# Scores of split vectors: a second pass over all 128 rows, and values split in every key block

## The chip, the cores and the metric

The kernel runs on one core of a Trainium2 chip. The metric is the device time of one execution in microseconds (us), smaller being better; the time before is the median of three runs.

## The reference, cut to what matters

The program is a two-layer encoder trunk with 512 tokens of 1024 features, all in float32. A layer is a feed-forward block, three token mixers that run on one normalised input and are merged by gates, and a second feed-forward block. The mixers are A (differential attention, 4 heads with two score products each), B (attention over a band of chunks with a table of biases, 8 heads) and C (retention, 4 heads with decay in place of softmax). The lines that the change touches compute the scores of A, B and C and the values of B:

```python
s = jnp.einsum('bqhcd,bkhcd->bhcqk', qi, k) * scale          # A, 4 heads x 2
s = jnp.einsum('bnqhd,bnkhd->bnhqk', qc, kb) * scale + bias  # B, 8 heads
o = jnp.einsum('bnhqk,bnkhd->bnqhd', p, vb)                  # B, values
inner = jnp.einsum('bnqhd,bnkhd->bnhqk', qc, kc) * decay     # C, 4 heads
```

Heads of q and k are 64 features wide; B's values are 64 wide, A's and C's 128.

## The kernel before, in words

**Split numbers.** Nearly all products run in a reduced float32 format (fp32r), and each operand is written as hi + lo to keep accuracy. A product of two split operands is three passes of TensorE (hi·hi, hi·lo, lo·hi). The large projections, the feed-forward blocks and the branch products go this way: one weight tile `wr` of 128x1024 arrives by DMA, ScalarE makes its hi (`wh`), VectorE its lo (`wl`), and 24 passes use the two. Three raw tiles and three split ones are in turn (RAW and SPL, lines 186 and 187). Where the diff has no say this is the "main program".

**Scores.** A head of q or k has only 64 features, and TensorE sums over up to 128 partitions, so hi and lo are stacked. `stack` (line 650; `c_prep`, line 996, for C) builds for each head a tile `qk` whose two halves of the partitions hold hi and lo of q, or hi twice for k, by DMAs from SBUF to SBUF on the queue of SyncE (SP). `dots` (line 664) then needs two passes. The first runs over all 128 rows and gives hi·hi + hi·lo. The second multiplies hi of q with lo of k; in the kernel before it takes one half of the partitions, 64 rows, straight from the tile `ql` that VectorE wrote (the tile `kl` in C). `scores` calls `dots` for a block of 128 queries with 256, 256, 384 and 512 keys in turn; C does the same with q and k exchanged.

**Values of B.** `evac_vb` (line 570) leaves the first three blocks of keys as pairs of tiles in which a head's hi and lo stand side by side (`vv`), the fourth as one tile in plain float32 (`v`). In `values_b` (line 591) the first three blocks take a pass 128 columns wide and one 64 columns wide; the fourth takes one plain float32 product with 64 columns of the values, which the trace records as two entries.

**What sets the order.** Heads and preparations are generators, "side programs". After each pass of the main program `tick` (line 249) may run one step of them. Which step is due is decided when the program is built, by `Model`, which estimates when each engine is through: a pass costs it n / 2.37 ns whatever its rows, a tile that DMAs fill counts as ready 2.5 us after `sent`, and a score waits 0.8 us more (`MARGIN`). Each engine and each queue then runs its own list in order. The requests for weights and the DMAs of `stack` share SP's queue. `b_head` for heads 0 and 1 starts once the first pair of k is sent, so its first scores come soon after those DMAs.

```python
    def dots(self, out, lhs, rhs):
        self.nc.tensor.matmul(out=out, lhsT=lhs[0], rhs=rhs[0], start=True, stop=False)
        self.nc.tensor.matmul(out=out, lhsT=lhs[1], rhs=rhs[1], start=False, stop=True)
```

Of the kernel before, what the change touches and what calls it, by code (L numbers as in the profile page):

```python
# [18 lines left out]
P = 128  # L19
S = 512  # L20
# [11 lines left out]
# columns of the per-partition constants  # L32
# [3 lines left out]
class Queue:  # L36
    """An engine's instructions, with an estimate of when each ends: side programs are woven in by it."""
# [14 lines left out]
class Model:  # L52
    """Estimates of when each engine is through with what it was given, and of which banks of PSUM are free."""
# [13 lines left out]
    def ready(self, ap, eng="pe"):  # L67
        """When an engine can read it."""
        end, by = self.wrote.get(self.key(ap), (0.0, eng))
        if by == eng:  # L70
            return end + (0 if eng == "pe" else 127)
        return end + self.LAG[by]
# [7 lines left out]
    def free(self, ap):  # L80
        """Its last reader is on the way."""
        end, by = max(self.read.get(self.key(ap), [(0.0, "pe")]))
        self.slots[self.owner.pop(self.key(ap))] = end + self.LAG[by]

    def sent(self, ap, wait=2500):
        """A transfer into it starts now."""
        self.wrote[self.key(ap)] = max(self.t.values()) + wait, "pe"
# [35 lines left out]
def then(*aps):  # L123
    """Wait: for a step of the vector or scalar engine."""
    return aps, False, 0


def product(*aps):
    """Wait: for a step of the tensor engine."""
    return aps, False, Kernel.EASE  # L130


def room(*aps):
    """Wait: for a step that takes a bank of PSUM."""
    return aps, True, Kernel.MARGIN


class Kernel:
# [26 lines left out]
    # ---------------------------------------------------------------- tiles  # L165
# [23 lines left out]
    # ------------------------------------------------- the stream of weights  # L189
# [39 lines left out]
    # ------------------------------------------------------- side programs  # L229
# [19 lines left out]
    def tick(self):  # L249
        """After a product of the main program: a step of a side program, where one is due."""  # L250
        m = self.model
        if self.late and m.ready(self.late[0][0], "dve") <= max(m.t["dve"], m.t["pe"]):
            self.late.pop(0)[1]()
        if self.prio and self.step(self.prio):
            return
        t = self.model.t
        if t["pe"] < self.due or max(t["dve"], t["act"]) > t["pe"] + self.BACKLOG:
            return
        self.admit()
        before = t["pe"]  # L260
        if self.step(self.active):
            self.due = t["pe"] + self.PACE * (t["pe"] - before)
# [17 lines left out]
    def step(self, lst):  # L280
        """Run the first program whose operands the tensor engine would not wait for."""
        for e in lst:
            if e[3] is not None and e[3] not in self.flags:
                continue
            if e[0] > self.model.t["pe"] or e[4] and min(self.model.slots) > self.model.t["pe"]:
                continue
            e[3] = None
            try:
                w = next(e[1])
            except StopIteration:  # L290
                lst.remove(e)
                return True
            if isinstance(w, str):
                e[3], e[4] = w, True
            else:
                aps, e[4], more = w
                e[0] = max([self.model.ready(a) for a in aps], default=0) + more
            return True
        return False
# [13 lines left out]
    # -------------------------------------------------------------- helpers  # L313
    def rsqrt(self, src, n, mul, add, final=None):
        """final / sqrt(src * mul + add), [P, n]."""
# [13 lines left out]
    def rsqrt_wide(self, y, src, mul, add, final=None):  # L329
        """y = final / sqrt(src * mul + add), [P, S], in steps."""  # L330
# [15 lines left out]
    def total(self, bank, parts):  # L346
        """Sums over the partitions, in every partition."""
        for i, x in enumerate(parts):
            self.nc.tensor.matmul(out=bank, lhsT=self.ones, rhs=x, start=i == 0, stop=i == 1)

    def split2(self, src, s):
        """hi and lo of a tile in SBUF."""
# [13 lines left out]
    # ------------------------------------------------------------- the norm  # L366
    def norm_part(self, k, gcol):
        """x[k] is final: its share of the sum of squares and its split for the next products."""
# [26 lines left out]
    def norm_rows(self):  # L395
        """rb, 1 / rms(x) by token in every partition."""
# [8 lines left out]
    def settle(self):  # L405
        """The urgent programs to their ends."""
# [4 lines left out]
    def norm_tokens(self):  # L411
        """rb, and rt with the tokens in partitions."""
# [10 lines left out]
    # ------------------------------------------------------------------ FFN  # L423
    def proj(self, xs, n=KD):
        """One output tile of features: a bank with its n products."""
# [7 lines left out]
    def open(self, xs):  # L433
        """The first two output tiles, side by side, as x and the weights come in."""
# [76 lines left out]
    # ---------------------------------------------------------------- mixer  # L511
    def tokens(self, evac, first=False):
        """512 columns of the projection with tokens in partitions."""
# [56 lines left out]
    def evac_vb(self, v):  # L570
        """The values of B: a head's hi and lo side by side."""
        nc = self.nc

        def f(b, bank):
            r = self.rt[:, b:b + 1]
            if b == NB - 1:
                t = self.big(F32, "v")
                nc.scalar.activation(out=t, in_=bank, func=AF.Copy, scale=r)
                v.append(t)
                return  # L580
# [10 lines left out]
    def values_b(self, pt, v, h):  # L591
        """A head's sum over the keys in the first half of a bank's partitions, but for the part of the values' lo, in the other."""
        o = self.bank()
        mm = self.nc.tensor.matmul
        for j in (0, 1, NB - 1, 2):
            if j == NB - 1:
                yield product(pt[j], v[j])
                mm(out=o[0:64, j * P:S], lhsT=v[j][:, h * 64:(h + 1) * 64], rhs=pt[j], start=False, stop=False)
                continue
# [10 lines left out]
    def prep(self, z, ms, out, flag, tabs=None, final=None, gain=None):  # L610
        """Norm and rotation of q or k (tokens in partitions), then the transposes and splits."""
# [38 lines left out]
    def stack(self, parts, out, flag):  # L650
        """Two heads of q or k, [2 * 64, tokens], split: for each head hi in its own half of the partitions
        and lo in the other (q), or hi twice (k), and what the second pass takes (hi of q, lo of k)."""
# [3 lines left out]
        for r, other in zip(half, half[::-1]):  # L656
            t = self.big(F32R, "qk")
            for o, x in ((r, hi), (other, lo if is_q else hi)):
                self.nc.sync.dma_start(out=t[o].bitcast(F32), in_=x[r].bitcast(F32))
            self.model.sent(t)  # L660
            out.append((t, (t if is_q else lo)[r]))
        self.flags.add(f"{flag}{len(out) // 2 - 1}")

    def dots(self, out, lhs, rhs):
        """Products of split vectors: of the stacked parts in one pass, of what is left in another."""
# [10 lines left out]
    def softmax(self, bank, i, add, s, e):  # L676
        """exp(scores + add - max) into e and the sums into s; add is [P, 512], aligned at its end."""
# [8 lines left out]
    def weights(self):  # L686
        """Room for the weights [q, k] of four blocks of queries."""
# [3 lines left out]
    def turned(self):  # L691
        """Room for the weights' transposes, by blocks of keys: [k, q], hi and lo."""
# [4 lines left out]
    def transposed(self, es):  # L697
        """Weights [q, k] of four blocks of queries -> per block of keys their transposes, split."""
# [20 lines left out]
    def values(self, pt, v, cols):  # L719
        """Sum over the keys: [values, queries] in a bank."""  # L720
# [10 lines left out]
    def settle_head(self, o, st, h):  # L731
        """A head's values out of PSUM, and the sums of their squares by token, in a half of the partitions."""
# [17 lines left out]
    def finish(self, st, heads, gains, final, gate, out, flag):  # L750
        """The norm over a head's values, its gains and its gate."""
# [134 lines left out]
    def table(self):  # L886
        """The next head's table of biases or decays."""
# [83 lines left out]
    def c_tables(self):  # L971
        """cos and sin, by the norm."""
# [6 lines left out]
    def rotated(self, tabs):  # L979
        """q or k of C, the first and the second halves of the four heads' features."""  # L980
# [15 lines left out]
    def c_prep(self, halves, out, s):  # L996
        """The split, and for each head hi in a half of the partitions and lo in the other (q), or hi twice (k),
        and what the second pass takes (hi of q, lo of k)."""
# [4 lines left out]
        for h in range(4):  # L1003
            hi, lo = ([p[i][32 * h:32 * h + 32] for p in parts] for i in range(2))
            t = self.big(F32R, "qk")
            a, b = h % 2 * 64, 64 - h % 2 * 64
            if s == "k" and h % 2 == 0:
                low = self.big(F32R, "kl")
            moves = [(t, a, hi), (t, b, hi if s == "k" else lo)]
            if s == "k":  # L1010
                moves.append((low, a, lo))
            for to, at, pieces in moves:
                for i, x in enumerate(pieces):
                    self.nc.sync.dma_start(out=to[at + 32 * i:at + 32 * i + 32].bitcast(F32), in_=x.bitcast(F32))
                self.model.sent(to)
            out.append((t, (low if s == "k" else t)[a:a + 64]))
# [64 lines left out]
    # ------------------------------------------------------------------ all  # L1081
# [132 lines left out]
```

## Time and profile before

| what | value |
|---|---|
| median of 3 runs | 2588.64 us (2587.83 to 2589.02) |
| span of the profiled execution | 2586.1 us |
| own time of the profiled execution | not given apart from the span; the median is 2.5 us above it |
| TensorE busy, passes | 2575.3 us, 11226 |
| VectorE busy | 1380.5 us, 53% |
| ScalarE busy | 921.3 us, 36% |
| granted TensorE clock, mean | 1.000 |

The span runs from the first to the last instruction. Matmuls overlap each other, and their ends are modelled, so a duration of a matmul is longer than the time that it keeps the next one waiting; the distance from start to start tells what a pass costs. A weight load (PEld) stands ahead of each pass and runs beside the pass before it where it can. In the timeline `128*64` behind an operation is rows times columns of the part of the array that is used, and `x2` a merged row.

### The profile page before, as it was taken

What the parts mean: (1) busy time and instruction counts of PE and PEld (TensorE: products, weight loads), DVE (VectorE), ACT (ScalarE), POOL (GpSimd) and SP (SyncE); (2) the same over time, 40 slices, a digit from 0 to 9 for tenths busy, and PEclk for the clock granted to TensorE, in tenths of its full rate; (3) what the DMA queues carried; (4) which work ended last, traced back from release to release, by engine and by line L of the source; (5) the groups of instructions that cost most, each with busy time, mean ns of one, the idle gap of its engine ahead of it and who ended that gap; (6) DMA issues with size and microseconds to landing.
All of it is one profiled execution on the core that took longest, in us unless ns stands there. A gap on an engine that the chain in (4) does not pass through costs nothing.

```text
span 2586.1 us, 28788 instructions
## 1 busy us (share of the span) xinstructions
PE 2575.3 (100%) x11226; PEld 2047.4 (79%) x11226; DVE 1380.5 (53%) x2176; ACT 921.3 (36%) x1395; POOL 133.8 (5%) x104
## 2 busy tenths in 40 slices
PE   9999999999999999999999999999999999999999
PEld 7888887777777888888888888877777778888887
DVE  6444347667658653343353343476776586544332
ACT  4333224544443333332232332245444433333321
POOL 0000101000102100000000001010001021000000
PEclk9999999999999999999999999999999999999999
DMA  4333335236422433333332323352364234333332
GB/s 164 98 94 94 118 118 142 78 86 157 121 81 82 131 98 98 98 98 92 97 97 90 98 90 118 113 151 70 89 161 122 71 90 130 98 94 94 98 110 70
DMA packets 90728, 271.46 MB, mean 105 GB/s; under 512 B 12256, under 2 KB 13664, under 8 KB 90592
## 3 DMA queue, kind: packets, MB, share of 16 engines
q1 hardware_dynamic: 89872, 269.01, 35.1%
q8 instruction: 88, 1.44, 0.2%
q10 hardware_dynamic: 720, 0.62, 0.1%
q14 instruction: 48, 0.39, 0.1%
HBM read 237.08 MB, written 6.29 MB: 94 GB/s over the span
## 4 chain that ended last, share of the span: by engine, by line
PE 99%; DVE 0%; DMA 0%; ACT 0%; issue 0%; SPq 0%
PE bank L48 99%; DVE z L48 0%; DMA x<-in_xt 0%; DMA w<-in_w 0%; ACT wh L48 0%; DVE xl L48 0%; DVE x L48 0%; DVE t L48 0%; ACT xh L48 0%; SPq L1109 0%; SPq L1107 0%; DVE wl L48 0%
## 5 line engine op out<-in xcount | busy, mean ns | idle before, releaser
L48 DVE TENSOR_TENSOR wl<-wr,wh 128x1024 fp32r<-128x1024 f32 x422 | 528.7, 1254 | 709.4 <-ACT wh L48 708.2
L48 PE MATMUL bank<-xh,wh 128*128 128x512 f32 x1920 | 762.3, 397 | 0.0
L48 PE MATMUL bank<-xh,wl 128*128 128x512 f32 x1920 | 759.2, 395 | 0.0
L48 PE MATMUL bank<-xl,wh 128*128 128x512 f32 x1920 | 757.1, 394 | 0.3 <-DVE xl L48 0.3
L48 ACT ACTIVATE wh<-wr 128x1024 fp32r<-128x1024 f32 x422 | 445.4, 1056 | 786.1 <-PE bank L48 674.5
L48 PEld LDWEIGHTS bank<-xh,wl 128*128 128x128 f32 x1920 | 361.2, 188 | 84.4 <-issue 3.8
L48 PEld LDWEIGHTS bank<-xl,wh 128*128 128x128 f32 x1920 | 361.3, 188 | 81.0 <-issue 2.2
L48 PEld LDWEIGHTS bank<-xh,wh 128*128 128x128 f32 x1920 | 361.5, 188 | 79.7 <-issue 1.8
L48 PE MATMUL bank<-ph,wh 128*128 128x512 f32 x704 | 277.6, 394 | 0.0
L48 PE MATMUL bank<-ph,wl 128*128 128x512 f32 x704 | 276.2, 392 | 0.0
L48 PE MATMUL bank<-pl,wh 128*128 128x512 f32 x704 | 275.9, 392 | 0.0
L48 PE MATMUL bank<-wh,xh 128*128 128x512 f32 x448 | 182.2, 407 | 0.0
L48 PE MATMUL bank<-wl,xh 128*128 128x512 f32 x448 | 181.9, 406 | 0.0
L48 PE MATMUL bank<-wh,xl 128*128 128x512 f32 x448 | 180.4, 403 | 0.0
L48 PEld LDWEIGHTS bank<-ph,wl 128*128 128x128 f32 x704 | 132.4, 188 | 30.6
L48 PEld LDWEIGHTS bank<-pl,wh 128*128 128x128 f32 x704 | 132.4, 188 | 29.1
L48 PEld LDWEIGHTS bank<-ph,wh 128*128 128x128 f32 x704 | 132.5, 188 | 28.8
L48 ACT ACTIVATE e<-e,m 128x128 f32<-128x128 f32 (+3 forms) x128 | 71.7, 560 | 136.4 <-DVE m L48 126.1
L48 ACT ACTIVATE t<-t 128x512 f32<-128x512 f32 x88 | 55.6, 632 | 162.4 <-DVE t L48 162.4
L48 PEld LDWEIGHTS bank<-wh,xh 128*128 128x128 f32 x448 | 84.2, 188 | 22.4 <-issue 4.3
L48 PEld LDWEIGHTS bank<-wh,xl 128*128 128x128 f32 x448 | 84.3, 188 | 20.4 <-issue 2.4
L48 PEld LDWEIGHTS bank<-wl,xh 128*128 128x128 f32 x448 | 84.4, 188 | 19.9 <-issue 2.1
(149 smaller groups left out, 2466.8 us busy)
## 6 DMA issues: line engine op xcount, KB each, us to landing
wr<-in_w SPq DMA_DIRECT2D x422, 512.0 KB, 3.5
qk<-qh SPq DMA_DIRECT2D x96, 128.0 KB, 4.6
xd<-x SPq DMA_DIRECT2D x16, 256.0 KB, 2.5
tb<-in_tbias SPq DMA_DIRECT2D x16, 256.0 KB, 3.8
qk<-ql SPq DMA_DIRECT2D x32, 128.0 KB, 4.3
rh<-r SPq DMA_DIRECT2D x32, 128.0 KB, 4.7
x<-xd SPq DMA_DIRECT2D x16, 256.0 KB, 5.3
qk<-yh SPq DMA_DIRECT2D x48, 64.0 KB, 2.0
```

What stands on the lines that cost most here:

```text
L48: return call(*args, **kw)
```

## The change

The second pass of the scores gets operands over all 128 partitions. For k, a second tile is built with lo in both halves, by two DMAs a head as for the first tile (in C four, where there were two into a tile shared by two heads). For q the whole tile is used, hi in one half and lo in the other. The pass then yields lo·hi + lo·lo in place of lo·hi. `twice` is new and holds what stood in the loop of `stack`. In B the fourth block of values is written as hi and lo side by side like the others, and its plain float32 product takes 128 columns in place of 64, so that the other half of the bank receives the part of lo. The order of all engines is worked out anew by `Model`. The diff also removes comments and docstrings, which shifts line numbers.

```diff
 def evac_vb(self, v):
...
-            if b == NB - 1:
-                t = self.big(F32, "v")
-                nc.scalar.activation(out=t, in_=bank, func=AF.Copy, scale=r)
-                v.append(t)
-                return
             two = [self.big(F32R, "vv") for _ in range(2)]
...
 def values_b(self, pt, v, h):
...
             if j == NB - 1:
-                yield product(pt[j], v[j])
-                mm(out=o[0:64, j * P:S], lhsT=v[j][:, h * 64:(h + 1) * 64], rhs=pt[j], start=False, stop=False)
+                t = v[j][h // 4][:, h % 4 * P:(h % 4 + 1) * P]
+                yield product(pt[j], v[j][h // 4])
+                mm(out=o[:, j * P:S], lhsT=t.bitcast(F32), rhs=pt[j], start=False, stop=False)
                 continue
...
 def stack(self, parts, out, flag):
...
         for r, other in zip(half, half[::-1]):
-            t = self.big(F32R, "qk")
-            for o, x in ((r, hi), (other, lo if is_q else hi)):
-                self.nc.sync.dma_start(out=t[o].bitcast(F32), in_=x[r].bitcast(F32))
-            self.model.sent(t)
-            out.append((t, (t if is_q else lo)[r]))
+            t = self.twice(hi[r], lo[r] if is_q else hi[r], r, other)
+            out.append((t, t if is_q else self.twice(lo[r], lo[r], r, other)))
         self.flags.add(f"{flag}{len(out) // 2 - 1}")
 
+    def twice(self, a, b, own, other):
+
+        t = self.big(F32R, "qk")
+        for o, x in ((own, a), (other, b)):
+            self.nc.sync.dma_start(out=t[o].bitcast(F32), in_=x.bitcast(F32))
+        self.model.sent(t)
+        return t
...
 def c_prep(self, halves, out, s):
...
-            t = self.big(F32R, "qk")
             a, b = h % 2 * 64, 64 - h % 2 * 64
-            if s == "k" and h % 2 == 0:
-                low = self.big(F32R, "kl")
-            moves = [(t, a, hi), (t, b, hi if s == "k" else lo)]
-            if s == "k":
-                moves.append((low, a, lo))
-            for to, at, pieces in moves:
-                for i, x in enumerate(pieces):
-                    self.nc.sync.dma_start(out=to[at + 32 * i:at + 32 * i + 32].bitcast(F32), in_=x.bitcast(F32))
-                self.model.sent(to)
-            out.append((t, (low if s == "k" else t)[a:a + 64]))
+            both = []
+            for one, two in ((hi, hi), (lo, lo)) if s == "k" else ((hi, lo),):
+                t = self.big(F32R, "qk")
+                for at, pieces in ((a, one), (b, two)):
+                    for i, x in enumerate(pieces):
+                        self.nc.sync.dma_start(out=t[at + 32 * i:at + 32 * i + 32].bitcast(F32), in_=x.bitcast(F32))
+                self.model.sent(t)
+                both.append(t)
+            out.append((both[0], both[-1]))
```

Two places of the order matter. The first is SP's queue where the k of A is stacked in the first layer (`wr` is a request for weights, `qh` and `ql` are hi and lo of a pair of heads, `x2` two DMAs). Before:

```order
L195 DMA wr_3098<-in_w 128x1024
L659 DMA qk_3151<-qh_3137 64x512 x2
L659 DMA qk_3154<-qh_3137 64x512 x2
L195 DMA wr_3180<-in_w 128x1024
L659 DMA qk_3191<-qh_3165 64x512 x2
```

Now:

```order
L195 DMA wr_3098<-in_w 128x1024
L661 DMA qk_3151<-qh_3137 64x512 x2
L661 DMA qk_3154<-ql_3138 64x512 x2
L661 DMA qk_3157<-qh_3137 64x512 x2
L661 DMA qk_3160<-ql_3138 64x512 x2
L195 DMA wr_3186<-in_w 128x1024
L661 DMA qk_3197<-qh_3171 64x512 x2
```

The pair takes eight DMAs in place of four ahead of the next request for weights, and the lo of the first head stands ahead of the hi of the second.

The second place is TensorE's list at the first scores of B's heads 0 and 1 in the first layer (`z` is normalised k that is transposed, `bank` with `xh`, `xl`, `yh`, `yl` is the main program). Before:

```order
L48 MATMUL bank_4763<-xl_2147,wh_4625 128x512
L48 MATMUL bank_4763<-xh_2146,wl_4626 128x512
L48 MATMUL bank_4763<-xh_2242,wh_4625 128x512
L48 MATMUL bank_4780<-qk_4691,qk_4392 128x256
L48 MATMUL bank_4780<-ql_4654,qk_4392 128x256
L48 MATMUL bank_4763<-xl_2243,wh_4625 128x512
L48 MATMUL bank_4763<-xh_2242,wl_4626 128x512
L48 MATMUL bank_4789<-qk_4694,qk_4395 128x256
L48 MATMUL bank_4789<-ql_4654,qk_4395 128x256
L48 MATMUL bank_4763<-xh_2338,wh_4625 128x512
```

Now:

```order
L48 MATMUL bank_4827<-xl_4708,wh_4690 128x512
L48 MATMUL bank_4827<-yh_4707,wl_4691 128x512
L48 MATMUL bank_4864<-qk_4755,qk_4505 128x256
L48 MATMUL bank_4864<-qk_4758,qk_4505 128x256
L48 MATMUL bank_4868<-yh_3935,wh_4690 128x512
L48 MATMUL bank_4868<-yl_3936,wh_4690 128x512
L48 MATMUL bank_4875<-qk_4761,qk_4508 128x256
L48 MATMUL bank_4875<-qk_4764,qk_4508 128x256
L48 MATMUL bank_4868<-yh_3935,wl_4691 128x512
```

The two heads still follow each other with two passes of the main program between them. What moved is the work around them (a branch product in place of a projection), and the second pass now reads a tile that a DMA fills.

## Rows read from the trace of the kernel before

**Rows 1.** The page: span, busy time and share by engine, the chain that ended last.
```profile
span 2586.1 us, 28788 instructions
...
PE 2575.3 (100%) x11226; PEld 2047.4 (79%) x11226; DVE 1380.5 (53%) x2176; ACT 921.3 (36%) x1395; POOL 133.8 (5%) x104
...
PE 99%; DVE 0%; DMA 0%; ACT 0%; issue 0%; SPq 0%
```

**Rows 2.** Waits of PE: us in total, times, longest us.
```profile
PE bank L48 <- DVE z L48: 3.5, 2, 1.7
...
PE bank L48 <- issue: 0.7, 1, 0.7
```

**Rows 3.** Groups by form, second passes: rows*columns, shape, count | busy us, mean ns.
```profile
L48 PE MATMUL bank<-ql,qk 64*128 64x256 f32 x64 | 24.4, 381 | 0.0
...
L48 PE MATMUL bank<-ql,qk 64*128 64x512 f32 x32 | 15.9, 498 | 0.0
...
L48 PE MATMUL bank<-ql,qk 64*128 64x384 f32 x32 | 14.0, 437 | 0.0
...
L48 PEld LDWEIGHTS bank<-qk,kl 64*128 64x128 f32 x32 | 5.8, 183 | 9.2 <-issue 9.2
```

**Rows 4.** Timeline of PE, main program alone: start us, length us, engine.
```profile
502.22 0.39 PE L48 MATMUL bank<-wl,xh 128*128 128x512 f32 x1
...
513.42 0.39 PE L48 MATMUL bank<-wl,xh 128*128 128x512 f32 x1
```

**Rows 5.** Timeline of PE, a score 256 keys wide.
```profile
449.43 0.28 PE L48 MATMUL bank<-qk,qk 128*128 128x256 f32 x1
...
450.52 0.39 PE L48 MATMUL bank<-wh,xh 128*128 128x512 f32 x1
```

**Rows 6.** Timeline of PEld, the same place.
```profile
449.63 0.18 PEld L48 LDWEIGHTS bank<-ql,qk 64*128 64x128 f32 x1 [0.24 <-issue]
```

**Rows 7.** Timeline of PE, scores 384 and 512 keys wide.
```profile
454.59 0.33 PE L48 MATMUL bank<-qk,qk 128*128 128x384 f32 x1
...
455.78 0.40 PE L48 MATMUL bank<-wh,xl 128*128 128x512 f32 x1
456.02 0.39 PE L48 MATMUL bank<-qk,qk 128*128 128x512 f32 x1
...
457.33 0.40 PE L48 MATMUL bank<-qk,qk 128*128 128x512 f32 x1
```

**Rows 8.** Timeline of PE, values of an A head, all over 128 rows.
```profile
484.50 0.52 PE L48 MATMUL bank<-pt,vh 128*128 128x384 f32 x2
...
485.26 0.27 PE L48 MATMUL bank<-ident,e 128*128 128x128 f32 x1
...
486.76 0.39 PE L48 MATMUL bank<-pt,vh 128*128 128x256 f32 x2
...
487.10 0.40 PE L48 MATMUL bank<-wh,xh 128*128 128x512 f32 x1
...
487.80 0.39 PE L48 MATMUL bank<-wh,xl 128*128 128x512 f32 x1
```

**Rows 9.** Timeline of PE, fourth key block of a B head's values.
```profile
643.37 0.39 PE L48 MATMUL bank<-yl,wh 128*128 128x512 f32 x1
...
644.39 0.40 PE L48 MATMUL bank<-pt,vv 128*64 128x256 f32 x2
```

**Rows 10.** Timeline of SP where the k of B is stacked.
```profile
609.53 7.71 SPq L659 DMA_DIRECT2D qk<-qh  x12
```

**Rows 11.** DMAs of that stack's first pair: count, KB each, us from issue to landing.
```profile
qk<-qh SPq DMA_DIRECT2D x4, 128.0 KB, 4.5
```

**Rows 12.** Timeline of PE, first score of B.
```profile
614.94 0.28 PE L48 MATMUL bank<-qk,qk 128*128 128x256 f32 x1
```

**Rows 13.** SP's DMAs in the stack of C: issue ns, shortest, median, longest.
```profile
L1014 SPq DMA_DIRECT2D qk<-yh x48: 535/586/1805, 678.4 to 1994.0; - x48
```

## The prediction

> **What bounds the kernel now.** The page comes first. TensorE is busy for the whole span and the chain that ended last lies on it for 99%; VectorE, the next busiest, is at 53% [rows 1]. The waits of PE come second: it waited twice for a normalised `z`, 3.5 us in all, and once for 0.7 us for nothing that the profile names [rows 2]. So time goes away only where TensorE gets less to do, or loses less between its passes.
>
> The groups by form come third, because "busy" hides such losses. The second passes of the scores use half of the array: 64 + 32 + 32 of them in A and B, and 32 in C, whose weight loads stand in the last row [rows 3]. That is 160 passes. By the widths of `scores` half of them are 256 keys wide, a quarter 384, a quarter 512: 80, 40 and 40. The groups give them a mean length (381 ns at 256 keys), but lengths of matmuls overlap, so I price them by starts in the timeline.
>
> The timeline comes fourth. Undisturbed, the main program starts a pass every 0.233 us (48 passes from 502.22 to 513.42) [rows 4]. Around a score it looks different: from the first pass of a score 256 wide to the start of the third pass of the main program behind it 1.09 us go by [rows 5]. The weight load of the 64-row pass sits idle for 0.24 us ahead of it and starts only at 449.63 [rows 6], 0.20 us behind the start of the pass before it, where loads between passes over 128 rows run beside the pass ahead.
>
> **The change, part by part.**
>
> *Second pass over 128 rows.* What a pair would cost if both passes used all rows is shown by A's values, which are the same format over 128 rows. Three passes of 256 columns take 487.10 - 486.76 = 0.34 us, 0.113 each; three of 384 and one of 512 take 0.76 us, so one of 384 takes (0.76 - 0.233) / 3 = 0.176 [rows 8].
> - 256 keys: 1.09 now [rows 5] against 2 x 0.113 + 2 x 0.233 = 0.69. Saved 0.40, 80 times: 32 us.
> - 384 keys: 455.78 - 454.59 = 1.19 [rows 7] against 2 x 0.176 + 2 x 0.233 = 0.82. Saved 0.37, 40 times: 15 us.
> - 512 keys: 457.33 - 456.02 = 1.31 [rows 7] against 4 x 0.233 = 0.93. Saved 0.38, 40 times: 15 us.
>
> The sum is 62 us, all on the path, since TensorE has no idle time that could swallow it. That the saving is nearly the same at each width says that it is a price of entering and leaving the half array, about 0.2 us each way, not of the columns. The difference of mean lengths would give a quarter of this; I don't take it, as the next pass of the main program starts late too, and only starts show that.
>
> The Trainium skill speaks against this term: the page "TensorE: Matmul & The Clock Gate", in the table of the section "Why this matters for your kernels", holds that a single matmul with 32 rows takes the same time as one with 128, so rows would not matter. By it this term would be nothing, and the time that of the second rival below. The trace disagrees by 0.37 to 0.40 us a pass, neighbours counted.
>
> *Fourth key block of B's values.* From the pass ahead of the plain float32 product to the second start behind it 644.39 - 643.37 = 1.02 us go by with 64 columns [rows 9]; the same sequence in A with 128 columns takes 487.80 - 487.10 = 0.70 [rows 8]. Saved 0.32 us, 8 heads in 2 layers: 5 us. The product keeps its format, so this is the columns alone. Splitting that block adds, in each layer, one step on ScalarE and two on VectorE, hidden as TensorE waits for neither there; if that cover went, it would be a few us at most.
>
> *The copies.* 64 more DMAs for the k of A and B and 16 for C go through SP's queue, ahead of requests for weights. One costs SP 0.64 us (12 in 7.71) [rows 10] and lands 4.5 us after its issue where B is stacked [rows 11]. Where heads start well after their stack this is hidden. It is not at B's heads 0 and 1. Now the fourth DMA of the pair, issued at 609.53 + 3 x 0.64 = 611.45, lands at about 615.95, and the first score starts at 614.94 [rows 12]. With eight DMAs the last lands at 609.53 + 7 x 0.64 + 4.5 = 618.5, and the pass that needs it, the second one of head 1, would stand 0.8 us behind the first score (three passes of 256 and two of 512), at 615.7. That is a wait of 2.8 us where there was none. The second layer has the same place, and the wait of 0.7 us for nothing named [rows 2] may be that place, already short. The model counts 2.5 us from `sent` however many DMAs there are, so it does not move the score back. I take 2.75 in each layer, 5.5 us. The low end is 0, if the stack's DMAs, which now stand behind a request for weights, get out earlier. The high end is 10, if A's first heads also wait 2 us in each layer. Five us of further issues in C delay weights whose raw and split tiles are six ahead; at 24 passes a tile that is 6 x 24 x 0.233 = 33 us of cover.
>
> *Waits that were covered.* The steps of softmax and transposes were placed by a model that never knew of the 0.4 us a score. Without it TensorE reaches the next transposes or values sooner, against VectorE at unchanged speed. Waits of PE are 4.2 us in all now. I take 1.5 more; the low end is 0, the high end 11, every other one of the 32 heads waiting 0.7 us as in [rows 2].
>
> **Sum.** 62 + 5 - 5.5 - 1.5 = 60 us. From the profiled span, 2586.1, that makes 2526.1; the median of the runs lies 2.5 above the span, and I keep that distance: **2528.6 us**. Were every cost at its low end, 67 us and 2521.6; the readings, rounded to 0.01 us, leave 3 us more, 2518.6. At the high ends 67 - 10 - 11 = 46, 2542.6, and again 3 us, 2545.6.
>
> **The rivals.**
>
> *Waits eat half.* The passes get cheaper, but every head then waits about once: 32 x 0.7 = 22 us, with the copies at 10. 67 - 32 = 35 us, 2553.6. For it: the slack of 0.4 us a score goes everywhere at once, and softmax runs through VectorE and ScalarE in turn. Against it: TensorE waits for them nowhere now but at the first `z`, and VectorE is idle for nearly half of the span. 0.10.
>
> *Rows do not matter.* The gap comes from something else that the second pass keeps, a switch between score and main program for instance. Then only B's values gain: 5 - 7 = -2, 2590.6, which is no change. For it: first passes and second passes alternate in every head, so no row shows a second pass of the scores over 128 rows. Against it: A's values enter and leave the main program with passes of the same widths and show no gap [rows 8]. 0.04.
>
> *Copies starve the weights: slower.* SP's queue runs in order, and in the stack of C 32 copies now stand between two requests for weights where 24 stood, in that of A's k 24 where 12 stood. At 0.64 us the longest hold is 20 us, within the 33 us of cover. The longest issue seen took 1.805 us [rows 13]; at that, C's would hold 58 us and A's 43, and 25 + 10 us would be lost in each layer, 70 in all: 2598.6. It decides from a mean of about 1.7 us a copy. The median there is 0.586, so this needs queues three times as slow. 0.03.
>
> **How the numbers follow.** A measurement of this kernel tells about 0.2%, 5 us, from no change. The forecast has 0.82, and the rest, 0.01, lies below its range. From 2518.6 to 2545.6 holds the forecast with both ends of its costs, nearly all of 0.82, so I give 2518 to 2546. Faster by over 0.2% are the forecast, the first rival and the rest: 0.93. Within 0.2% is the second: 0.04. Slower is the third: 0.03.
>
> **What would show it.** In the groups by form the 64-row passes are gone and 160 more `qk` passes appear at the mean lengths of the first ones. Starts around a score 256 wide lie at 0.69 in place of 1.09 us. The loads ahead of second passes have no idle time put down to issue. B's fourth block shows 1.02 turning into 0.70. At B's first scores PE, or its weight load, waits some 2 to 3 us for a DMA into `qk`. The prediction is wrong if starts around second passes stay where they are, or if PE's waits grow beyond 20 us; then the list of waits must name VectorE, ScalarE or that DMA.

## The result, and the profile after

The changed kernel takes **2550.2 us** (median of 4 runs, 2546.87 to 2552.31); the kernel before, on the same chip, 2588.36. The ratio is 0.9853, 95% interval 0.9839 to 0.9867. It is faster by 38 us, where 60 were forecast, and its time lies above the range of 2518 to 2546.

The page of the kernel after: span, busy time, the chain that ended last by engine and by line.

```profile
span 2550.4 us, 28931 instructions
...
PE 2517.2 (99%) x11226; PEld 2054.4 (81%) x11226; DVE 1375.7 (54%) x2180; ACT 919.8 (36%) x1397; POOL 138.3 (5%) x104
...
PE 93%; DVE 3%; SPq 2%; DMA 1%; issue 0%; ACT 0%; DVEq 0%
PE bank L48 93%; SPq L661 1%; SPq L1012 1%; DVE wl L48 1%; DMA qk<-ql 1%; DVE e L48 0%; DMA x<-in_xt 0%; DVE n L48 0%; DVE g L48 0%; DVE z L48 0%; DVE pt L48 0%; DVE r L48 0%; DMA qk<-yh 0%; DVE ql L48 0%; ACT wh L48 0%
```

TensorE lost 58 us of busy time against [rows 1], but the span fell by 36 only. The chain, 99% PE before, now leaves PE for 7%, and first among the lines it goes to are SP's issues of L661 (`twice`) and L1012 (`c_prep`). The waits of PE after (us in total, times, longest us):

```profile
PE bank L48 <- DVE e L48: 17.4, 6, 5.2
PE bank L48 <- DMA qk<-ql: 3.5, 6, 0.8
PE bank L48 <- DVE z L48: 3.4, 2, 1.7
PE bank L48 <- DVE warm L48: 1.5, 1, 1.5
PE bank L48 <- DMA qk<-qh: 1.4, 4, 0.6
```

Beside the `z` of [rows 2] stand two new ones: `e`, the softmax weights that VectorE hands over for the transposes, 17.4 us, and the copies themselves, 4.9 us. Why VectorE is late shows in what it and ScalarE wait for; not one such row exists for the kernel before:

```profile
DVE e L48 <- DMA qk<-ql: 16.9, 4, 6.0
ACT v L48 <- DMA qk<-yh: 16.1, 2, 8.1
DVE vl L48 <- DMA qk<-yh: 14.7, 2, 7.4
ACT e L48 <- DMA qk<-ql: 13.5, 3, 6.7
ACT qh L48 <- DMA qk<-qh: 7.0, 2, 3.7
DVE e L48 <- DMA qk<-qh: 4.2, 2, 2.2
DVE wl L48 <- DMA qk<-yl: 0.9, 1, 0.9
```

These seven rows add to 73.3 us. Read the first: `e` reads a bank and a table, no `ql`. It waits for a DMA that *reads* `ql`. All large tiles share a ring of slots (`RING = 72`, line 184). When the program is built, a tile is given a slot whose last tile has no use left further down in the program; on the chip such a use can still be to come. In the program as built, the `e` that starts at 623.58 below lies in the slot of the very `ql` whose copies it waits for, 13 tiles after it in the order of first writes. If the slot's last tile is the source of a copy which has not run, the writer waits, and with it everything behind it on its engine. SP's queue at the stack of B's k (start us, length us):

```profile
603.97 1.11 SPq L661 DMA_DIRECT2D qk<-qh  x2
605.19 1.16 SPq L661 DMA_DIRECT2D qk<-ql  x2
...
622.97 1.20 SPq L661 DMA_DIRECT2D qk<-qh  x2
624.25 1.19 SPq L661 DMA_DIRECT2D qk<-ql  x2
```

Thirty-two copies take 603.97 to 625.4, where sixteen stood. VectorE at that time (in brackets: idle before, and its releaser):

```profile
617.27 0.29 DVE L48 TENSOR_SCALAR e<-e,s 128x128 f32<-128x128 f32 x1
623.58 0.42 DVE L48 CUSTOM_DVE_ANT_0 e<-bank,tb 128x256 f32<-128x256 f32 x1 [6.03 <-DMA qk<-ql]
```

And TensorE, which gets its `e` late:

```profile
627.73 0.27 PE L48 MATMUL bank<-ident,e 128*128 128x128 f32 x1
628.95 0.33 PE L48 MATMUL bank<-ident,e 128*128 128x128 f32 x1 [0.94 <-DVE e L48]
631.89 0.46 PE L48 MATMUL bank<-ident,e 128*128 128x128 f32 x1 [2.61 <-DVE e L48]
...
633.00 0.63 PE L48 MATMUL bank<-yh,wh 128*128 128x512 f32 x1
633.42 0.63 PE L48 MATMUL bank<-yl,wh 128*128 128x512 f32 x1
```

The stops are not all. After them passes start 0.42 to 0.43 us apart in place of 0.233. The granted clock by stretch (length, PE busy and passes, clock, DMA share, GB/s) tells why:

```profile
629.00:633.00 4.00, 1.39 (x5) 0.87 0.41 122
633.00:637.00 4.00, 4.00 (x19) 0.71 0.61 197
637.00:641.00 4.00, 4.00 (x22) 1.00 0.40 113
```

Behind the two stops the clock fell to half, 1.2 GHz, for some 3 us (0.87 and 0.71 are means of both levels) and came back. Over the span 24 passes of 512 columns started 0.43 us apart, which is 24 x 0.196 = 4.7 us.

The stack of C's k repeats this with a longer hold. The eight groups of four copies run from 690.78 to 711.2; VectorE and ScalarE stand still before `vl` and `v`:

```profile
709.23 0.75 DVE L48 SCALAR_TENSOR_TENSOR vl<-bank,rt,vh 128x512 fp32r<-128x512 f32 x1 [7.31 <-DMA qk<-yh]
709.89 0.15 DVE L48 RECIPROCAL s<-s 128x1 f32<-128x1 f32 x1
710.08 0.49 DVE L48 TENSOR_SCALAR e<-e,s 128x512 f32<-128x512 f32 x1
```

```profile
709.93 0.69 ACT L48 ACTIVATE v<-bank,rt 128x512 f32<-128x512 f32 x1 [8.05 <-DMA qk<-yh]
```

```profile
710.63 0.47 PE L48 MATMUL bank<-ident,e 128*128 128x128 f32 x1 [5.10 <-DVE e L48]
```

`vl` and `v` lie in the slots of the two `yh` (hi of C's k), 28 and 25 tiles after them, and the copies of the last head still read those. The copies of lo stand between those of hi in the queue, so they delay them. The reciprocal and the `e` behind `vl` do not need that slot; they wait because VectorE takes its list in order. The second layer has the same three stops of TensorE.

### The profile page after: what moved, and what is told of

Same layout as the page of the kernel before. It is cut to its first block, busy times and chain, and to the rows that moved or that the text cites. A ratio compares the mean times of both kernels' runs of the same rounds, so it can differ in the third digit from the quotient of the medians.

```text
span 2550.4 us, 28931 instructions
## 1 busy us (share of the span) xinstructions
PE 2517.2 (99%) x11226; PEld 2054.4 (81%) x11226; DVE 1375.7 (54%) x2180; ACT 919.8 (36%) x1397; POOL 138.3 (5%) x104
## 4 chain that ended last, share of the span: by engine, by line
PE 93%; DVE 3%; SPq 2%; DMA 1%; issue 0%; ACT 0%; DVEq 0%
PE bank L48 93%; SPq L661 1%; SPq L1012 1%; DVE wl L48 1%; DMA qk<-ql 1%; DVE e L48 0%; DMA x<-in_xt 0%; DVE n L48 0%; DVE g L48 0%; DVE z L48 0%; DVE pt L48 0%; DVE r L48 0%; DMA qk<-yh 0%; DVE ql L48 0%; ACT wh L48 0%
## 5 line engine op out<-in xcount | busy, mean ns | idle before, releaser
L48 POOL TENSOR_TENSOR acc<-acc,sq 128x512 f32<-128x512 f32 x30 | 39.4, 1314 | 1112.1 <-PE bank L48 567.7
```

The lines of the kernel that those rows point to most:

```text
L48: return call(*args, **kw)
```

## The experiments

Eleven kernels ran, each beside runs of the kernel before on the same chip (medians 2587.15 to 2589.12). One thing must be known to read the times. The plain stream of passes has two paces, a little different, and a whole feed-forward block keeps one. The first such block of the second layer in the profiles of the kernel after and of e2 below:

```profile
1400.00:1500.00 100.00, 100.00 (x430) 1.00 0.33 95
```

```profile
1400.00:1500.00 100.00, 100.00 (x439) 1.00 0.32 96
```

430 or 439 passes in 100 us at a granted clock of 1.00: over the block's 1584 passes that is some 7 us. The profiles of before, after, e1, e7c, e8 and e10 have the slow pace there; those of e2, e3, e4, e5, e7, e9 and e9b the quick one. One kernel's runs spread by as much and more (the kernel before from 2577.4 to 2589.6 in the first comparison); what pace the runs without a profile had is not known. I compare profiles with that 7 us taken off where their paces differ, and read nothing into medians that differ by less than 7 us.

**The first four, in one comparison.** My theory: the rows and the values give what was forecast, and the copies of lo take some 30 us back. Rivals: the cover of softmax is gone, or the rows give less.

*Values alone (e1).* The kernel before with the edits of `evac_vb` and `values_b` only.

```diff
-            if b == NB - 1:
-                t = self.big(F32, "v")
...
-                mm(out=o[0:64, j * P:S], lhsT=v[j][:, h * 64:(h + 1) * 64], rhs=pt[j], start=False, stop=False)
+                mm(out=o[:, j * P:S], lhsT=t.bitcast(F32), rhs=pt[j], start=False, stop=False)
```

> Only the fourth key block of B's values is changed; the scores and their copies stay as they were. By the starts in the timeline (1.02 against 0.70 us, 16 times) the kernel before should lose 5 us: 2583, and the gap around that product should read 0.70 as in A. If the 64 columns were not what costs, nothing moves: 2588.

2575.92 us (2572.68 to 2582.28), ratio 0.996, 0.9938 to 0.9983. The profiled span is 2578.1, 8.0 below before's 2586.1 at the same pace, where 5 were forecast.

*Rows without copies (e2).* The second pass over 128 rows, reading the first tile of k again; the scores leave out lo of k.

```diff
-            out.append((t, t if is_q else self.twice(lo[r], lo[r], r, other)))
+            out.append((t, t))
...
-            for one, two in ((hi, hi), (lo, lo)) if s == "k" else ((hi, lo),):
+            for one, two in ((hi, hi),) if s == "k" else ((hi, lo),):
```

> As the changed kernel, but lo of k is not copied at all: the second pass runs over all 128 rows of the first tile again, so the scores leave out the products with lo of k and count the others twice. Theory (the copies): the passes are as cheap as predicted, 62 + 5 us, and what was missing comes from the copies, so 2521 to 2524, with DVE and ACT waiting for no DMA into qk. Rival (the cover): softmax falls behind a faster TensorE whoever copies, so 2545 to 2552, with the same waits of PE for e, some 17 us. Rival (the rows): the passes themselves gain less, 2540 or more with no such waits.

2511.81 us (2511.55 to 2518.45), ratio 0.9713, 0.9698 to 0.9727. This is below the range of the theory. PE waits for `z`, as before, and 1.5 us for copies of hi; `e` does not appear, and neither VectorE nor ScalarE waits for a copy. So neither the cover nor the rows fell short. From e1 the span falls by 68.1, less 7 for the pace 61: the 62 us of the row term.

*Copies without the rows (e3).* The copies of the change, but the second pass over one half of them.

```diff
-            out.append((t, t if is_q else self.twice(lo[r], lo[r], r, other)))
+            out.append((t, (t if is_q else self.twice(lo[r], lo[r], r, other))[r]))
...
-            out.append((both[0], both[-1]))
+            out.append((both[0], both[-1][a:a + 64]))
```

> As the changed kernel with all its copies, but the second pass uses one half of the stacked tiles, 64 rows as before. It has the order and the queues of the changed kernel and none of the gain of the rows. Theory (the copies): 2583 and on top of it most of the 30 us that were missing, 2600 to 2615, with DVE and ACT waiting for DMAs into qk as in the changed kernel. Rival (the cover): with the slow passes back the slack is back too, 2583 to 2590.

2602.08 us (2595.11 to 2605.56), ratio 1.0052, 1.0035 to 1.0069: slightly slower than before, and 26 us slower than e1 by the medians. By the profiles, 2593.3 (quick pace) and 2578.1 (slow), it is 22 us at the same pace. The waits of VectorE and ScalarE on copies are back (seven rows, 65.3 us), as are PE's for `e`. The longest of the seven, and PE's:

```profile
DVE e L48 <- DMA qk<-ql: 18.9, 4, 7.2
PE bank L48 <- DVE e L48: 13.7, 6, 3.8
```

So the copies do most of this alone, with slow second passes too. The rest, up to the 33.5 us of the kernel after (worked out below), came only together with the faster passes; why is not shown.

*Another way to the same operand (e5).* Lo of k is not copied: GpSimd multiplies the pair's lo tile by a column that is 1 in one half of the partitions and 0 in the other, so the second pass runs over 128 rows and adds lo·hi alone.

```diff
-            out.append((t, t if is_q else self.twice(lo[r], lo[r], r, other)))
+            out.append((t, t if is_q else self.masked(lo, i)))
...
+    def masked(self, lo, i):
+        t = self.big(F32R, "qm")
+        self.nc.gpsimd.tensor_scalar(out=t, in0=lo.bitcast(F32), scalar1=self.halves[i], scalar2=1.0, op0=ALU.mult, op1=ALU.mult)
+        return t
```

In C the pieces of two heads' lo go into one tile by DMAs, as in the kernel before, and are masked there.

> Second pass over 128 rows without any new DMA: GpSimd multiplies lo of a pair of heads by a column that is one in one half of the partitions and zero in the other, and that tile meets the stacked q (hi and lo), so that hi times lo remains and the rest is times zero. SP's queue has the copies of the kernel before. Theory (the copies): 2521 to 2530, no waits of DVE or ACT for DMAs into qk. Rival (the cover): about 2550, PE waiting for e. Rival (the ring of tiles): a tile more for each head is live here as in the changed kernel, and if that and not the time in the queue makes the waits, they stay but name POOL.

**2520.44 us** (2520.31 to 2522.51), ratio 0.9742, 0.9727 to 0.9757. The waits of VectorE and ScalarE on copies are 17.3 us in five rows, in place of 73.3; PE waits 7.5 us for `e`. None were expected. These are waits for copies that the kernel before has too, of hi and of C's lo into `kl`: in another order of slots those hold up writers as well. So the rival of the ring is right in part, though only one row, 1.2 us, names POOL.

**Is it the queue, or the slots?**

*Another queue (e4).* The change, with the copies of lo issued on GpSimd's queue.

```diff
-            out.append((t, t if is_q else self.twice(lo[r], lo[r], r, other)))
+            out.append((t, t if is_q else self.twice(lo[r], lo[r], r, other, self.nc.gpsimd)))
...
-            self.nc.sync.dma_start(out=t[o].bitcast(F32), in_=x.bitcast(F32))
+            (eng or self.nc.sync).dma_start(out=t[o].bitcast(F32), in_=x.bitcast(F32))
...
-                        self.nc.sync.dma_start(out=t[at + 32 * i:at + 32 * i + 32].bitcast(F32), in_=x.bitcast(F32))
+                        (self.nc.gpsimd if one is lo else self.nc.sync).dma_start(out=t[at + 32 * i:at + 32 * i + 32].bitcast(F32), in_=x.bitcast(F32))
```

> The change as it is, with the copies of lo of k issued from GpSimd's DMA queue in place of SP's; the instructions of the four engines' own work and the tiles are the same. Theory queue: what costs is that a copy waits its turn in SP's queue (20.5 us for the 32 copies of C's k), and so holds its source tile; then the waits of VectorE and ScalarE on copies (51 us in the changed kernel by its groups of waits) go below 15 us, PE's waits for e from 17 to below 8 us, and the time is 2520 to 2532 us. Theory transfers: the copies themselves are slow, whatever queue; the time stays at 2545 to 2555 us. A third case: the issues cost GpSimd more than SP's 0.6 us each, its own work (squares, multiplications) comes late, and the time is 2535 to 2550 us with waits of PE for POOL in place of those for e.

2539.15 us (2533.56 to 2539.68), ratio 0.9809, 0.9795 to 0.9824. The waits of VectorE and ScalarE on copies fell to 13.5 us (from 73.3; the 51 above left rows out) and PE's for `e` to 3.0, as the queue theory has it, but the time stayed above its 2532. Something else came up, the first row of PE's waits:

```profile
PE bank L48 <- DMA qk<-qh: 10.2, 6, 3.2
PE bank L48 <- DVE z L48: 3.4, 2, 1.7
PE bank L48 <- DVE e L48: 3.0, 2, 1.5
```

Two queues now send at once, and the copies land later, those of hi too. DMAs from 600 to 630 us (count, KB each, median us to landing):

```profile
qk<-ql POOLq DMA_DIRECT2D x16, 128.0 KB, 6.4
qk<-qh SPq DMA_DIRECT2D x16, 128.0 KB, 6.4
```

In the kernel after, from 603 to 626 us, these take 3.8 and 4.3. B's first scores wait for hi of k. The DMA engines have no room there. The last two numbers of these rows are their busy share and GB/s, in the kernel after and in e4:

```profile
606.00:626.00 20.00, 17.20 (x78) 13.28 (x77) 8.34 (x21) 5.24 (x12) 0.00 (x0) 1.00 1.00 244
606.00:626.00 20.00, 15.35 (x65) 12.14 (x64) 9.37 (x21) 5.50 (x11) 6.86 (x14) 0.83 0.98 236
```

So at the stack of B's k the second queue shortens SP's line but moves no more bytes, and the theory of transfers is right in part. At the stack of C's k in the kernel after the share is 0.51 (691 to 711 us), and there it is the line that holds the sources. GpSimd's own work being late, the third case, is not what cost: PE does not wait for POOL.

*More slots (e7, and its control e7c).* The change with 75 slots; to make room for them, two buffers of raw weights in place of three. The control has the two buffers and 72 slots.

```diff
-    RING = 72
+    RING = 75
...
-    RAW = 3
+    RAW = 2
```

> The change with three more slots in the ring of large tiles (75 for 72), paid for with one buffer of raw weights less (2 for 3); to be held against the control with 72 slots and the same two buffers. Theory ring: a copy that has not run costs only because its source holds the slot that the next tile is to be written into; with three slots more the writers come to a slot that was freed earlier, the waits of VectorE and ScalarE on copies fall from 51 us by at least half, and the time is 10 to 25 us below the control. Theory lateness: the first score waits for its copy whatever the ring, and the time is that of the control, within 4 us.

> Control: the change with two buffers of raw weights in place of three, 72 slots. Every weight request is made one piece later. If the third buffer was spare, 2546 to 2556 us as the change; if the requests between the copies need it, PE waits for weights (rows of PE on in_w, none in the changed kernel) and the time is 2556 to 2580 us.

75 slots: 2534.13 us (2531.33 to 2541.16), ratio 0.98, 0.978 to 0.9821. Control: 2555.01 us (2549.12 to 2557.2), ratio 0.9872, 0.9856 to 0.9887. The control is where it was expected if the third buffer is spare. That is 21 us between the medians; the profiled spans, 2532.1 and 2555.2, have the two paces, which leaves 16. The waits of VectorE and ScalarE on copies go from 64.8 (control) to 39.7 us, not quite the half that was expected. So slots matter, but three are not enough.

*Do slots help anyway (e10)?* The same two edits in the kernel before.

> Control: the kernel before with 75 slots and two buffers of raw weights. Theory ring (the slots cost only because copies of lo hold them): before shows no wait of VectorE or ScalarE on a copy, so the slots give nothing and the fewer weight buffers cost 0 to 5 us: 2585 to 2593 us. If 75 slots are of use by themselves, whatever the copies: 2560 to 2575 us, and the 21 us between the two kernels with two buffers are not the copies'.

2578.52 us (2575.91 to 2584.45), ratio 0.9957, 0.994 to 0.9974. That is in neither range, and the interval excludes 1. The profiled span is 2582.5 at before's pace, 3.6 less than 2586.1, and PE's wait for `z` fell from 3.5 to 1.3. So slots help a little without copies of lo, by 3.6 us, or by up to 8.4 if the lost raw buffer costs here the 4.8 us that it costs in the control (2555.2 against 2550.4, the same pace). Of the 16 us, 8 to 12 are then the copies'.

**Both cures, and what is best.**

*Other queue and 75 slots, e8* (the diffs of e4 and e7 together).

> The two cures at once: the copies of lo of k in GpSimd's queue, and 75 slots of the ring with two buffers of raw weights. If both take away the same waits (of VectorE and ScalarE on tiles that a copy holds), the gains do not add up: 2525 to 2534 us, near the better of the two alone (2534.13 and 2539.15 us) less what the other queue spares the first heads. If they take away different waits, about 11 and 21 us off the control's 2555 us: 2520 to 2525 us.

2534.56 us (2529.13 to 2537.83), ratio 0.9792, 0.9768 to 0.9816, a little above the range given for gains that do not add up. The profiled span, 2535.7, has the slow pace; at the quick one it is some 3 us below those of e4 and e7 (2531.8 and 2532.1). One wait of 0.2 us on a copy is left to VectorE and none to ScalarE, and the time is still close to that of one cure alone: PE waits 8.2 us for hi of k at the first scores. What is left there is mainly not slots but copies that land late.

*Masked lo and 75 slots, e9* (those of e5 and e7).

> The masked lo without copies of its own (2520.44 us), with 75 slots and two buffers of raw weights. It still shows 7.5 us of PE waiting for e and 11 us of VectorE on tiles that copies hold. Theory ring: three slots more take these away, and the clock's drop behind them: 2508 to 2517 us. If the two buffers of raw weights cost their 4 us (the control against the change) and the ring has nothing left to give: 2522 to 2527 us.

**2509.72 us** (2508.84 to 2510.33), ratio 0.9703, 0.9686 to 0.9719: the fastest, 40 us below the kernel after. Its page and PE's waits:

```profile
PE 2497.2 (100%) x11226; PEld 2047.7 (82%) x11226; DVE 1374.3 (55%) x2180; ACT 920.0 (37%) x1397; POOL 172.7 (7%) x148
```

```profile
PE bank L48 <- DVE warm L48: 1.5, 1, 1.5
PE bank L48 <- DVE z L48: 1.3, 2, 0.6
PE bank L48 <- DVE yl L48: 0.9, 2, 0.4
PE bank L48 <- DMA qk<-qh: 0.8, 2, 0.6
```

`e` is gone, and one row of waits on copies is left, 3.8 us of VectorE.

*Masked lo and 73 slots, e9b*, all that fits beside three raw buffers.

```diff
-    RING = 72
+    RING = 73
```

> The masked lo with 73 slots and the three buffers of raw weights, all that fits beside them. Theory ring: one slot moves every writer one tile, so part of what 75 slots give: 2512 to 2520 us; without effect it stays at 2520 us.

2524.54 us (2523.5 to 2525.7), ratio 0.976, 0.9743 to 0.9777: nothing gained; a miss. PE waits 8.7 us for `e`. With one slot more the tiles fall into other slots, and `vl` and `v` come to wait for copies in both layers (7.2 and 8.4 us), where e5 had one such wait on each engine (4.5 and 4.2).

## Why the prediction was wrong, point by point

The passes of the main program are the same in the kernel after and in e2, so the distance between their starts shows where the copies' price arises. At the end the kernel after is 40.4 us behind. Of these 1.0 and 0.6 arise at A's scores (layers 1 and 2), 15.3 and 16.6 in B and C (some 8 to 9 at the stack of B's k and 7 at that of C's in each layer), and 6.9 in the feed-forward block of the other pace, which is no part of the change. The copies cost the rest, **33.5 us**.

- **Second pass over 128 rows: right.** Forecast 62. The starts around all second passes, in the profiles of before and after, give 62.9, and e1 against e2 61. In the kernel after the form has its row (busy us, mean ns, idle before), and the timeline shows a score 256 wide with its surroundings:

```profile
L48 PE MATMUL bank<-qk,qk 128*128 128x256 f32 x160 | 34.4, 289 | 5.0 <-DMA qk<-ql 3.5 <-DMA qk<-qh 1.4
```

```profile
450.81 0.40 PE L48 MATMUL bank<-qk,qk 128*128 128x256 f32 x2
...
451.52 0.39 PE L48 MATMUL bank<-wh,xh 128*128 128x512 f32 x1
```

  From the score to the third pass behind it are 451.52 - 450.81 = 0.71 us, against 1.09 in [rows 5] and 0.69 forecast. The price is that of the half array in rows. Passes of split numbers on half of the columns do not pay it: in B a pass over 64 columns and one over 128, both 384 wide, take 646.76 - 646.40 = 0.36 together (the merged row gives the form of the first), twice the 0.176 of [rows 8]. The plain float32 product does pay on 64 columns, 0.34 us by the next point. The Trainium skill, page "TensorEngine Tiling (Array Packing)", section "Key Properties", says that a change of the tiling mode drains TensorE. The 64-row passes agree, at 0.39 us in and out; the 64-column passes of split numbers show no drain, and why the plain ones cost more no run here tells.

```profile
646.40 0.52 PE L48 MATMUL bank<-pt,vv 128*64 128x384 f32 x2
646.76 0.39 PE L48 MATMUL bank<-xl,wh 128*128 128x512 f32 x1
...
647.22 0.39 PE L48 MATMUL bank<-xh,wh 128*128 128x512 f32 x1
647.45 0.38 PE L48 MATMUL bank<-pt,vv 128*128 128x128 f32 x2
...
647.90 0.40 PE L48 MATMUL bank<-pt,vv 128*64 128x256 f32 x2
```

- **Fourth key block of B's values: right.** 647.90 - 647.22 = 0.68, forecast 0.70, where [rows 9] had 1.02. That is 5.4 us of 5; e1's span fell by 8.0.
- **The copies: the step that failed.** Forecast 5.5, at most 10; measured 33.5. What I looked at came true: B's heads 0 and 1 wait for their copies (2.3 and 2.1 us in the two layers, where 2.75 each were forecast), and PE's weight requests have their cover (no wait of PE on weights). What failed is the sentence "where heads start well after their stack this is hidden". It asked only when the copy's *result* is needed. A copy also holds its *source* until it has run, and with 16 more copies at 0.64 us in the queue that is 10 us more for the last ones. The next writer of that slot waits, on an engine that runs in order, whatever it writes and for whom. The page shows none of this before the change; what could have been read is the length of the queue (16 more copies at 0.64 us) and, in the program as built, which tiles are given the slots of the copies' sources.
- **Waits that were covered: right.** Forecast 1.5 of loss. With rows at full speed and no copies of lo, all waits of PE add to 7.5 us in e2 and 5.8 in e9, against 6.0 in the kernel before (the 4.2 of the prediction left out 1.5 for `warm` at the start and 0.3 more).
- **The rivals.** "Waits eat half" gave 2553.6, which is close to the result, by another cause: not every head waits once for want of cover; PE stops at three places a layer where VectorE and ScalarE were held by copies. "Rows do not matter" fell. "Copies starve the weights" had the right place, SP's queue during the stacks, and the wrong victim.

Together, at the same pace: 2586.1 - 62.9 - 5.4 + 33.5 = 2551.3 us against the measured span of 2550.4. That copies of lo bring it is shown by e2, which has none of them and none of the 33.5, and by e9, which computes lo rightly without copies of its own and spans 2507.5 us against e2's 2510.0; e3 shows 22 us of it with the old passes. What stays open is how the 33.5 divide between slots that are held, results that are late and DMA engines that are full. The two cures overlap, and the run with both (e8) has the lateness of its two queues.

## What to carry to other kernels

A DMA that is hidden for its reader still holds its source. Before adding copies to a queue, list who writes next into the slots of their sources, in the order of the queue, and price the stop of that whole engine. Where an idle engine can make the operand in place (here GpSimd, 40 masks, 31 us of its time), it takes no place in the queue and holds its source for less long (0.7 us a mask; in e9 ScalarE waited 5.9 us for masks, and PE for none). And a ring is tuned as a whole: with the masks three slots more, paid for with a weight buffer, gave 11 us (e9 against e5), and one slot none (e9b).

## What the runs showed of the hardware that was not expected

- Two paces of an undisturbed stream at a granted clock of 1.00: 430 or 439 passes of 512 columns in 100 us, kept for a whole block, in different runs of like kernels. No run here tells what chooses between them.
- A stop of TensorE can be paid for twice. Around each of the four stops of 2.6 to 5.2 us in the kernel after the granted clock, at 1.00 until then, fell to half for some 3 to 4 us of passes (0.43 us from start to start in place of 0.23). It is not sure to: in e3 two stops of 2.6 us, and in e7 one of 3.1 us, left the clock at 1.00. No run here tells which stops do.
- DMAs from SBUF to SBUF on two queues at once landed 6.4 us after their issue, against about 4 on one queue, with the DMA engines busy for 0.98 and 1.00 of the time: the second queue shortened the line, not the landing.
- A split (fp32r) pass over 64 of the 128 rows cost 0.39 us beside full passes, one over 64 of the 128 columns nothing; a plain float32 product cost 0.34 us more over 64 columns than over 128.
